# Moving state-space parameters, squares and states in the mixer of a hybrid decoder layer

## The chip, the cores and the metric

The kernel runs on one core of a Trainium2 chip. The metric is the device time of one execution in microseconds; the times shown are medians of several runs.

## The reference

One decoder layer on 1024 tokens of width 1024, in float32. A vector c gives six modulation rows; x is normalized and modulated, and `proj = hn @ w_in` feeds two mixers side by side, gated linear attention (GLA) and a diagonal state-space model (S5). A mixture of experts (4 of 32) follows.

```python
mod = jax.nn.silu(c) @ ada_w[l] + ada_b[l]
sh1, sc1, g1, sh2, sc2, g2 = jnp.split(mod, 6, axis=-1)
hn = rmsnorm(h, mix_pre_g[l]) * (1.0 + sc1[:, None, :]) + sh1[:, None, :]
proj = hn @ w_in[l]
q, k, v, og, a_lr, u = jnp.split(proj, SPLITS, axis=-1)
...
# s5_layer(u, ...): per group of 16 channels, 64 complex states
dt = jnp.exp(log_dt)[:, None]
mag = jnp.exp(lr * dt)
ab_re = mag * jnp.cos(li * dt); ab_im = mag * jnp.sin(li * dt)
...
_, _, xr, xi = lax.associative_scan(combine, (a_re, a_im, bu_re, bu_im), axis=1)
y = einsum(xr, c_re) - einsum(xi, c_im) + d * uf
y = jax.nn.gelu(y); s5 = y * jax.nn.sigmoid(y @ glu_w + glu_b)
...
h = h + g1 * rmsnorm(jnp.concatenate([gla, s5]) @ w_out, mix_post_g)
h = h + g2 * rmsnorm(moe_ffn(rmsnorm(h, ffn_pre_g) * (1 + sc2) + sh2), ffn_post_g)
```

## The kernel before, in words

Every engine runs its instructions in the order in which the program issues them, and so do the queues from which SP, ACT and POOL issue transfers; semaphores hold an instruction until what it reads is there and until what it overwrites has been read. The tile `S` is one large buffer which `view` cuts into places by hand; many places serve several things one after the other.

**Modulation rows.** `ada_row(i, mod_c, on_v)` (line 289) is a generator. Each of its eight steps issues one load of 512 KB from SP into the next of six buffers (`ada_r`, line 240) and uses it: TensorE multiplies it by c (`product`, four passes), or, for the k listed in `on_v`, VectorE multiplies it into `acc` (line 306 for the first, line 308 for the others; helpers at 143 and 148), which TensorE sums later. A last step turns the row into columns. `rows[0]` has `on_v` = (2, 5), `rows[1]` has (1, 3, 5). Load number n waits until load n - 6 has been used; the ninth load (the first of `rows[1]`) follows the use of k = 2 of `rows[0]` on VectorE. `take(gen, n)` (line 650) advances a generator by n steps. After the loads of the rows SP issues x's blocks 0 to 3, `fetch(0)` (1 MB of w_in), `load_b`, x's blocks 4 to 7 and smaller loads.

**State-space parameters.** `s5_prep` (line 360) is a generator of nine steps of small VectorE operations (128x16): the exponential of dt, angle and exponential, sine and cosine, powers of the rotation (`u8a`, the end of step 4), and so on. `s5_rot` (line 480) builds the rotation tables `rot` from `u8a` with POOL, doubling the width n from 1 to 64; the last stage has twelve operations of 128x512. Lines 133, 136 and 139 are the helpers for multiplication, addition and subtraction on VectorE and POOL alike.

**x.** `x_half(q)` (line 730) takes four blocks of x, squares them on ACT with accumulators (line 733), and VectorE makes 1/rms (ten small operations) and the diagonal matrices `dg`. `x_cols(q, k)` (line 739) lets TensorE transpose and scale a column block with `dg` (line 744), ACT writes it twice (lines 747 and 748), and VectorE subtracts the low part (`hnl`). `tile_T(i, j, half, first)` (line 754) is a tile of 24 matmuls of 128x512 (line 768) on high and low parts; with `first` it calls `x_cols` for all eight k between its matmuls. `u_tile` (line 776) evacuates such a tile and, after the second half, writes it to `U_d` from ACT. The order is `u_tile(0,0,0,first)`, `x_half(1)`, `u_tile(0,1,0)`, `u_tile(0,0,1,first)`, `conv(1)`, `u_tile(0,1,1)`, `load_u(0)`, `u_tile(1,0,0)`, `u_tile(1,1,0)`, `u_tile(1,0,1)`, `u_tile(1,1,1)`, `load_u(1)`. `load_u` (line 784) reloads U from `U_d` from SP in another layout, eight transfers.

**The planner.** The order between these tiles and side work is made while the program is built, by counted costs. `now` is TensorE's planned time, `busy` VectorE's; `spend(us)` advances `now` and lets background generators (`background(gen, at)`) go on if they are due and `busy` is less than `look` ahead. A generator yields "v" (it costs VectorE so much), "pe" (TensorE), "lag" and "sync" (not before so much later). `finish(...)` issues all the rest of a generator at once, without regard to its lags. Side work is: `s5_g` (line 510: for each of eight h8, six multiplications and additions of 128x256 on VectorE, then transposes on TensorE), `s5_ca` (line 529: eight steps, each with a complex multiplication on VectorE into `ca`, four CA_d writes from SP, copies on ACT, products on TensorE into `kr` by a copy on ACT, eight T_d writes from SP; `ca` and `kr` exist once), and `s5_states(hf)` (line 573: for q = 0, 1: 32 products with U on TensorE (line 584), six operations on VectorE in the places r1, r2, zr, zi of C1, scans (line 599), six more, and four XY writes from SP (line 610) that read r1 and zi). `states(0)` starts 5 us of planned time after `u_tile(1,0,0)`; its end is forced by `finish(st_a)` (line 862), ahead of the gates (lines 867 to 900) and the k tiles. `finish(g_gate, g_m, g_st)` (line 975) issues what is left of `s5_ca` and `states(1)` ahead of the q tiles. `s5_outs` (line 621) makes four output groups and is ended by `finish(g_y)` (line 986).

```python
    def pump():
        ...
                while g[1] <= now[0] and busy[0] < now[0] + look[0] and step(g):
    ...
            st_a = states(0)
            background(st_a, now[0] + 5.0)
        u_tile(1, 1, half)
    load_u(1)
```

Of the kernel before, what the change touches and what calls it, by code (L numbers as in the profile page):

```python
# [16 lines left out]
AF = mybir.ActivationFunctionType  # L17
OP = mybir.AluOpType
# [7 lines left out]
EPS = 1e-6  # L26
RD = 1.0 / 32.0
# [21 lines left out]
def hybrid_layer_kernel(ctx: ExitStack, tc: tile.TileContext, I, out):  # L49
    nc = tc.nc  # L50
    V, A, P, PE, SP = nc.vector, nc.scalar, nc.gpsimd, nc.tensor, nc.sync
# [16 lines left out]
    def carve(base, kb, *dims):  # L68
        n = 1
        for d in dims:  # L70
            n *= d
        o = int(round(kb * 256))
        v = base[:, o:o + n]
        if len(dims) == 2:
            v = v.rearrange("p (a b) -> p a b", a=dims[0])
        elif len(dims) == 3:
            v = v.rearrange("p (a b c) -> p a b c", a=dims[0], b=dims[1])
        return v

    def view(kb, *dims, dt=F32):  # L80
        n = 1
        for d in dims:
            n *= d
        o = int(round(kb * 256))
        w = n if dt in (F32, F32R, I32, U32) else n // 2
        assert o + w <= int(SBKB * 256), (kb, dims)
        v = S[:, o:o + w]
        if dt != F32:
            v = v.bitcast(dt)
        if len(dims) == 2:  # L90
            v = v.rearrange("p (a b) -> p a b", a=dims[0])
        elif len(dims) == 3:
            v = v.rearrange("p (a b c) -> p a b c", a=dims[0], b=dims[1])
        elif len(dims) == 4:
            v = v.rearrange("p (a b c d) -> p a b c d", a=dims[0], b=dims[1], c=dims[2])
        return v
# [12 lines left out]
    def small(*dims, dt=F32):  # L109
        n = 1  # L110
        for d in dims:
            n *= d
        kb = small_at[0]
        small_at[0] += n / 256
        return view(kb, *dims, dt=dt)
# [7 lines left out]
    def trb(*dims):  # L123
        return bank("tr", 2, *dims)

    def axb(*dims):
        return bank("ax", 3, *dims)
# [13 lines left out]
    def ts(o, a, s1, op0, s2=None, op1=None, e=None):  # L141
        if op1 is None:
            (e or V).tensor_scalar(o, a, s1, None, op0=op0)  # L143
        else:
            (e or V).tensor_scalar(o, a, s1, s2, op0=op0, op1=op1)

    def stt(o, a, s, b, op0, op1, **kw):
        V.scalar_tensor_tensor(o, a, s, b, op0=op0, op1=op1, **kw)  # L148

    def bc(ap, axis, n):  # L150
        u = ap.unsqueeze(axis)
        shape = list(u.shape)
        shape[axis] = n
        return u.to_broadcast(shape)
# [9 lines left out]
    now, busy, look = [0.0], [0.0], [LOOK]  # L164
# [34 lines left out]
    def background(gen, at=0.0):  # L199
        gens.append([gen, at])  # L200
# [15 lines left out]
    TB = 64  # L216
# [132 lines left out]
    def cmul(o, x, y, t, neg_im=False, e=None):  # L349
        mul(t[0], x[0], y[0], e)  # L350
        mul(t[1], x[1], y[1], e)
        sub(o[0], t[0], t[1], e)
        mul(t[0], x[0], y[1], e)
        mul(t[1], x[1], y[0], e)
        if neg_im:
            stt(o[1], t[0], -1.0, t[1], OP.mult, OP.subtract)
        else:
            add(o[1], t[0], t[1], e)
# [121 lines left out]
    def s5_rot():  # L480

        for hf in range(2):
            for i in range(2):
                P.memset(rot[hf][i][:, :, 0:1], 1.0 - i)
        wk, wn, t16 = u8a, [small(16), small(16)], [small(16), small(16)]
        n = 1
        while n < 128:
            for hf in range(2):
                tr4 = [carve(C1, 2 * i, 8, n) for i in range(2)]
                gl = slice(8 * hf, 8 * hf + 8)  # L490
                ro = rot[hf]
                cmul([ro[i][:, :, n:2 * n] for i in range(2)], [ro[i][:, :, 0:n] for i in range(2)],
                     [bc(wk[i][:, gl], 2, n) for i in range(2)], tr4, e=P)
            if 2 * n < 128:
                cmul(wn, wk, wk, t16, e=P)
                wk, wn = wn, wk
            n *= 2
# [123 lines left out]
    def s5_outs():  # L621
        y8 = [C1[:, 1024 * i:1024 * i + 1024].rearrange("p (a b c) -> p a b c", a=4, b=2)
              for i in range(2)]

        load_tc(1)
        yield "lag", 2.0
        for Q in range(4):
            hf = Q // 2
            for g2 in range(2):
                yp = axb(4, 128)  # L630
                for j in range(4):
                    gl = 2 * j + g2
                    PE.matmul(yp[:, j], T8[Q % 2][:, gl], U16[:, 8 * Q + gl], start=True, stop=False)
                    PE.matmul(yp[:, j], C8[Q % 2][:, gl], XY[hf][g2][:, 4 * (Q % 2) + j], start=False, stop=True)
                A.activation(y8[Q % 2][:, :, g2], yp, AF.Gelu_apprx_tanh)
                yield "pe", 1.8
            for t_ in range(8):
                A.dma_start(bass.AP(tensor=Y_d.tensor, offset=Y_d.offset + Q * 128 * 1024 + t_ * 128,
                                    ap=[[1024, 16], [16384, 8], [1, 128]]),
                            y8[Q % 2][16 * t_:16 * t_ + 16].rearrange("p a b n -> p (a b) n"))  # L640
            yield "lag", 1.5
            if Q < 2:
                load_tc(Q + 2)
            yield "lag", 1.0 if Q == 0 else 3.0


    mod = small(16)
    prep = s5_prep()

    def take(gen, n=1):  # L650
        for _ in range(n):
            try:
                next(gen)
            except StopIteration:
                return
# [5 lines left out]
    vecs2 = view(TB + 2.5, 128)  # L661
    for nm, r_, n in (("s5_glu_b", 0, 4), ("b_alpha", 4, 2), ("gla_norm_g", 6, 1)):
        P.dma_start(vecs2[r_:r_ + n], I[nm][0].rearrange("(a b) -> a b", b=128))
    take(prep)
    take(rows[0], 5)
    take(prep)
    p0 = trb(24)
    PE.transpose(p0, vecs[0:24], ident[0:24, 0:24])
    V.tensor_copy(vt, p0)
# [4 lines left out]
    glub, balpha, glag = vt2[:, 0:4], vt2[:, 4:6], vt2[:, 6:7]  # L674
    take(rows[0], 2)
    take(rows[1], 2)
    take(prep)
    take(rows[0])
    a1 = small(8)
    stt(a1, mod[:, 8:16], 1.0, vt[:, 16:24], OP.add, OP.mult)  # L680
    take(prep)
    s5_rot()
    X0, X1 = slot("E0"), slot("E1")
    xa = [view(R2 + 4 * b, 1024) for b in range(4)] + [carve(X0, 0, 1024), carve(X0, 4, 1024), carve(X1, 0, 1024),
                                                       carve(X1, 4, 1024)]
# [35 lines left out]


    sst, rx, tx, hx_ = small(8), small(8), small(8), small(8)
    dg = view(R0 + 14, 4, 128)
    hx_r = [view(TB, 512), view(TB + 2, 512)]
    hnh = [t_[:, 0:1024] for t_ in HN]
    hnl = [t_[:, 1024:2048] for t_ in HN]
    n_hx = [0]

    def x_half(q):  # L730
        c4 = slice(4 * q, 4 * q + 4)
        for b in range(4 * q, 4 * q + 4):
            A.activation(view(TB, 1024), xa[b], AF.Square, scale=RD, accum_out=sst[:, b:b + 1])
        ts(sst[:, c4], sst[:, c4], EPS, OP.add)
        rsqrt(rx[:, c4], sst[:, c4], tx[:, c4], hx_[:, c4])
        mul(dg, bc(ident, 1, 4), bc(rx[:, c4], 2, 128))
        vec(2.0)

    def x_cols(q, k):
        cols = slice(512 * q, 512 * q + 512)  # L740
        n_hx[0] += 1
        pt = (trb, axb)[n_hx[0] % 2](4, 128)
        for b in range(4):
            PE.matmul(pt[:, b], xa[4 * q + b][:, k * 128:(k + 1) * 128], dg[:, b], start=True, stop=True)
        pt = pt.rearrange("p a b -> p (a b)")
        hx = hx_r[n_hx[0] % 2]
        A.activation(hx, pt, AF.Identity, bias=mod[:, k:k + 1], scale=a1[:, k:k + 1])
        A.activation(hnh[k][:, cols], pt, AF.Identity, bias=mod[:, k:k + 1], scale=a1[:, k:k + 1])
        sub(hnl[k][:, cols], hx, hnh[k][:, cols].bitcast(F32))
        vec(0.6)  # L750
        spend(0.87)


    def tile_T(i, j, half, first=False):

        hi, lo = wparts[i]
        o = mmb(512)
        cols = slice(512 * half, 512 * half + 512)
        c_ = slice(128 * j, 128 * j + 128)
        n = 0  # L760
        if first:
            for k in range(3):
                x_cols(half, k)
        for k in range(8):
            if first and k < 5:
                x_cols(half, k + 3)
            for a_, b_ in ((hi, hnh), (hi, hnl), (lo, hnh)):
                PE.matmul(o, a_[:, k, c_], b_[k][:, cols], start=(n == 0), stop=(n == 23))
                n += 1
            if k % 2:  # L770
                spend(1.3)
        return o
# [75 lines left out]
    for half in range(2):  # L848
        u_tile(1, 0, half)
        if half == 0:  # L850
            conv(2)
            fetch(3)
            st_a = states(0)
            background(st_a, now[0] + 5.0)
        u_tile(1, 1, half)

    load_u(1)
# [583 lines left out]
    for blk in range(2, 8):  # L1441
        oo, xt = [mmb(512), axb(512)], load_x(blk)
        routes.append(route(blk, oo, xt))
        q = blk - 1
# [574 lines left out]
```

## Time and profile before

| | |
|---|---|
| median of 3 runs | 2021.15 us (2018.4 to 2021.25) |
| the profiled execution, its own time | 2024.69 us |
| its span, first to last instruction | 2022.9 us |
| busy share of the span | PE 89%, weight loads 80%, DVE 76%, ACT 59%, POOL 26% |
| mean granted TensorE clock | 0.948 of full speed |
| DMA | 540.82 MB, mean 267 GB/s |

Times in the rows below are microseconds from the span's start; of one instruction in a group some are given in ns. PE is TensorE's matmul row, DVE VectorE, ACT ScalarE, POOL GpSimd, and SPq the queue from which SP issues transfers (its durations are those of the issue, not of the transfer). A line of the timeline merges instructions that follow each other: start, time, engine, line, operation, what it writes and reads, how many, and in brackets the idle time of the engine before it and what ended it.

### The profile page before, as it was taken

Reading aid. Unit: us, or ns where it says so; the run is one execution under the profiler, and the core shown is the slowest. Engines: PE = TensorE matmul, PEld = TensorE weight load, DVE = VectorE, ACT = ScalarE, POOL = GpSimd, SP = SyncE. Lnnn points to the kernel's source line nnn. Section 1 sums busy time; section 2 is a strip of 40 time slices with the busy share of each in tenths; the row PEclk is TensorE's granted clock in tenths of the full one; section 3 lists DMA queues with packets and bytes.
Section 4 is the critical chain, followed back from the end, with each engine's and each line's share of the span. In section 5 each row is a group of like instructions: output and inputs, shape, how many; then the busy total and the mean of one; then the engine's idle time right before and its main releaser. Section 6 shows DMA issues by size and latency. Waiting matters only on the chain. (4 is left out here: it accounts for less than half of the span.)

```text
span 2022.9 us, 53263 instructions
## 1 busy us (share of the span) xinstructions
PE 1806.0 (89%) x22354; PEld 1614.5 (80%) x22354; DVE 1544.2 (76%) x2396; ACT 1199.1 (59%) x1682; POOL 526.5 (26%) x495
## 2 busy tenths in 40 slices
PE   8678699998968999998998899999899889999970
PEld 3566588787858999998998899767799789999870
DVE  5766537568767997995997799689799868869835
ACT  3524133544226876875776677577688667768641
POOL 4720012203543025015104402400330330160043
PEclk8889899999978999999999899999999989999985
DMA  9176465323359999999999899888999999999874
GB/s 310 39 193 132 137 196 161 126 70 131 115 172 326 363 322 353 379 351 307 323 329 358 278 351 341 279 323 301 299 367 365 301 296 330 327 318 350 306 192 175
DMA packets 296804, 540.82 MB, mean 267 GB/s; under 512 B 41234, under 2 KB 66032, under 8 KB 296528
## 3 DMA queue, kind: packets, MB, share of 16 engines
q1 hardware_dynamic: 259504, 469.51, 67.5%
q0 software_dynamic: 30384, 60.49, 11.8%
q10 hardware_dynamic: 6672, 7.38, 1.1%
q8 instruction: 177, 2.90, 0.6%
q14 instruction: 67, 0.55, 0.1%
HBM read 489.57 MB, written 45.61 MB: 265 GB/s over the span
## 5 line engine op out<-in xcount | busy, mean ns | idle before, releaser
L1765 POOL DMA_INDIRECT ff_d<-A,S x102 | 260.7, 2555 | 353.8 <-DVE A L143 141.2
L1588 DVE SCALAR_TENSOR_TENSOR B<-A,B 128x2048 f16<-128x2048 f32 x110 | 249.5, 2285 | 33.1 <-ACT B L1585 21.0
L1588 DVE SCALAR_TENSOR_TENSOR E<-A,E 128x2048 f16<-128x2048 f32 x110 | 249.7, 2285 | 16.0 <-ACT E L1585 15.8
L1726 POOL DMA_INDIRECT S<-hn_d,S x51 | 77.8, 1526 | 702.2 <-PE tr L1736 661.7
L1588 DVE SCALAR_TENSOR_TENSOR C<-A,C 128x2048 f16<-128x2048 f32 x110 | 249.7, 2284 | 8.3 <-ACT C L1585 8.2
L1585 ACT ACTIVATE B<-A 128x2048 f16<-128x2048 f32 x110 | 209.2, 1917 | 46.7 <-DMA A<-in_exp_w_gu_dram 36.7
L1585 ACT ACTIVATE E<-A 128x2048 f16<-128x2048 f32 x110 | 208.9, 1917 | 33.1 <-DMA A<-in_exp_w_gu_dram 18.4
L1585 ACT ACTIVATE C<-A 128x2048 f16<-128x2048 f32 x110 | 208.7, 1920 | 25.9 <-PE ax L1792 15.3
L1791 PE MATMUL mm<-S,E 128*128 128x92 f16 (+29 forms) x1336 | 187.8, 230 | 0.6 <-issue 0.5
L1791 PE MATMUL mm<-S,B 128*128 128x164 f16 (+28 forms) x1364 | 185.3, 227 | 3.3 <-issue 3.2
L1792 PE MATMUL mm<-S,B 128*128 128x164 f16 (+28 forms) x1364 | 184.9, 227 | 3.8 <-issue 3.8
L1792 PE MATMUL mm<-S,E 128*128 128x92 f16 (+29 forms) x1336 | 187.5, 229 | 0.0
L1792 PE MATMUL mm<-S,C 128*128 128x92 f16 (+28 forms) x1352 | 183.0, 226 | 3.2 <-issue 3.0
L1791 PE MATMUL mm<-S,C 128*128 128x92 f16 (+28 forms) x1352 | 183.2, 227 | 1.7 <-ACT S L1602 1.7
L1791 PEld LDWEIGHTS <-B 128*128 128x128 f16 x1760 | 154.3, 98 | 16.8 <-issue 9.4
L1791 PEld LDWEIGHTS <-C 128*128 128x128 f16 x1760 | 153.3, 98 | 13.0 <-issue 6.3
L1791 PEld LDWEIGHTS <-E 128*128 128x128 f16 x1760 | 155.0, 98 | 9.6 <-issue 2.0
L1792 PEld LDWEIGHTS <-B 128*128 128x128 f16 x1760 | 154.2, 98 | 9.4 <-issue 2.1
L1792 PEld LDWEIGHTS <-E 128*128 128x128 f16 x1760 | 154.9, 98 | 7.9 <-issue 0.4
L1792 PEld LDWEIGHTS <-C 128*128 128x128 f16 x1760 | 153.0, 98 | 8.3 <-issue 1.8
L148 DVE SCALAR_TENSOR_TENSOR S<-S 128x1 f32<-128x1 f32 (+7 forms) x249 | 106.0, 434 | 42.2 <-DMA S<-in_ada_w_dram 28.4
L1588 DVE SCALAR_TENSOR_TENSOR A<-A,A 128x2048 f16<-128x2048 f32 x54 | 123.5, 2286 | 3.1 <-ACT A L1585 2.9
(353 smaller groups left out, 4266.7 us busy)
## 6 DMA issues: line engine op xcount, KB each, us to landing
A<-in_exp_w_gu_dram SPq DMA_DIRECT2D x256, 1024.0 KB
A<-in_exp_w_down_dram SPq DMA_DIRECT2D x128, 1024.0 KB
S<-in_ada_w_dram POOLq DMA_DIRECT2D x64, 256.0 KB
S<-in_ada_w_dram SPq DMA_DIRECT2D x16, 512.0 KB
S<-in_w_in_dram SPq DMA_DIRECT2D x8, 1024.0 KB
S<-in_x_dram SPq DMA_DIRECT2D x12, 512.0 KB
ff_d<-S POOLq DMA_DIRECT2D x18, 256.0 KB
S<-in_w_out_dram SPq DMA_DIRECT2D x8, 512.0 KB
```

The costliest lines, as they stand in the source:

```text
L148: V.scalar_tensor_tensor(o, a, s, b, op0=op0, op1=op1, **kw)
L1585: A.activation(WH[n % NWS], ST[n % NST], AF.Copy, scale=WS)
L1588: V.scalar_tensor_tensor(WL[n % NWS], ST[n % NST], WS, WH[n % NWS], op0=OP.mult, op1=OP.subtract, accum_out=acc_col())
L1726: lambda e: P.indirect_dma_start(out=x_[0:cb], out_offset=None, in_=hn2_d, in_offset=bass.IndirectOffsetOnAxis(ap=x.lt[0:cb, b, 0:1], axis ...
L1765: lambda e: P.indirect_dma_start(out=ff_d[c], out_offset=bass.IndirectOffsetOnAxis(ap=x.lt[0:cb, b, 0:1], axis=0), in_=yt[0:cb], in_offset ...
L1791: PE.matmul(pp[q], w_, mh[:, f_], start=(f_ == 0 and q % per == 0), stop=False, skip_group_check=True)
L1792: PE.matmul(pp[q], w_, ml[:, f_], start=False, stop=False, skip_group_check=True)
```

## The change

Steps 2 to 4 of `s5_prep` and `s5_rot` are issued ahead of the steps of `rows[0]` that follow its first load. The squares of x's blocks 4 to 7 become eight half squares with accumulators of their own (`sst2`), issued on ACT behind the last `x_cols` of the first tile, with `hnh[7]`'s second half as their scratch; `x_half(1)` adds the two halves. `states(0)` starts 16 us of planned time after `u_tile(1,0,0)`. The lag behind the second output group of `s5_outs` is 10 instead of 3.

```diff
@@ s5_outs
-            yield "lag", 1.0 if Q == 0 else 3.0
+            yield "lag", (1.0, 10.0, 3.0, 3.0)[Q]
@@
-    take(prep)
+    take(prep, 4)
+    s5_rot()
     take(rows[0], 5)
-    take(prep)
     p0 = trb(24)
...
     take(rows[0], 2)
     take(rows[1], 2)
-    take(prep)
     take(rows[0])
     a1 = small(8)
     stt(a1, mod[:, 8:16], 1.0, vt[:, 16:24], OP.add, OP.mult)
-    take(prep)
-    s5_rot()
@@
+    sst2 = small(2, 4)
...
+    def x_squares():
+
+        for b in range(4, 8):
+            for i in range(2):
+                A.activation(hnh[7][:, 512:1024], xa[b][:, 512 * i:512 * i + 512], AF.Square, scale=RD,
+                             accum_out=sst2[:, i, b - 4:b - 3])
+
     def x_half(q):
         c4 = slice(4 * q, 4 * q + 4)
-        for b in range(4 * q, 4 * q + 4):
-            A.activation(view(TB, 1024), xa[b], AF.Square, scale=RD, accum_out=sst[:, b:b + 1])
-        ts(sst[:, c4], sst[:, c4], EPS, OP.add)
+        if q:
+            stt(sst[:, c4], sst2[:, 0], EPS, sst2[:, 1], OP.add, OP.add)
+        else:
+            for b in range(4):
+                A.activation(view(TB, 1024), xa[b], AF.Square, scale=RD, accum_out=sst[:, b:b + 1])
+            ts(sst[:, c4], sst[:, c4], EPS, OP.add)
@@ tile_T
             if first and k < 5:
                 x_cols(half, k + 3)
+            if first and half == 0 and k == 4:
+                x_squares()
@@
             st_a = states(0)
-            background(st_a, now[0] + 5.0)
+            background(st_a, now[0] + 16.0)
```

## Rows read from the trace of the kernel before

**Rows 1.** Busy time by stretch: engines, granted clock, DMA share, GB/s; the start.

```profile
0.00:22.60 22.60, 17.61 (x37) 3.27 (x37) 10.28 (x61) 2.49 (x4) 2.76 (x13) 1.00 0.86 308
22.60:34.60 12.00, 11.00 (x33) 3.46 (x34) 9.26 (x50) 4.15 (x8) 4.90 (x15) 0.86 1.05 386
```

**Rows 2.** Timeline, TensorE: the first products on x.

```profile
42.28 2.08 PE L744 MATMUL ax<-S 128*128 128x128 f32 x8
```

**Rows 3.** Timeline, SP's queue: loads of the modulation's weights, merged and one alone.

```profile
2.43 11.63 SPq L300 DMA_DIRECT2D S<-in_ada_w_dram  x9
...
12.53 0.33 SPq L300 DMA_DIRECT2D S<-in_ada_w_dram  x1
```

**Rows 4.** Groups of instructions, POOL, 75.2 to 92.1 us: count, busy us, mean ns.

```profile
L133 POOL TENSOR_TENSOR C<-E,S 128x512 f32<-128x512 f32 x8 | 10.3, 1310 | 0.2
```

**Rows 5.** Groups, VectorE, 81.5 to 89.4 us and 102 to 115 us.

```profile
L133 DVE TENSOR_TENSOR S<-S 128x256 f32<-128x256 f32 x4 | 5.2, 1347 | 0.0
...
L133 DVE TENSOR_TENSOR S<-S 128x256 f32<-128x256 f32 x16 | 6.1, 421 | 0.2
```

**Rows 6.** Timeline, 28 to 98 us: rotation, squares, second half, its evacuation.

```profile
28.78 0.21 POOL L133 TENSOR_TENSOR C<-E,S 128x8 f32<-128x8 f32 x1 [25.28 <-DVE S L139]
...
62.14 1.05 ACT L733 ACTIVATE S<-E 128x1024 f32<-128x1024 f32 x1
...
66.86 0.18 DVE L143 TENSOR_SCALAR S<-S 128x4 f32<-128x4 f32 x1 [3.07 <-ACT S L733]
...
71.79 1.28 PE L744 MATMUL ax<-S,E 128*128 128x128 f32 x8 [4.26 <-DVE S L133]
...
97.61 0.60 ACT L158 ACTIVATE S<-mm 128x512 f32<-128x512 f32 x1 [3.99 <-PE mm L768]
```

**Rows 7.** Busy time by stretch: U's reload, and its second half with XY.

```profile
120.60:132.00 11.40, 0.01 (x2) 0.03 (x1) 3.11 (x9) 1.94 (x5) 0.00 (x0) 0.64 1.18 178
162.00:174.50 12.50, 11.56 (x64) 8.94 (x63) 7.29 (x14) 9.47 (x13) 0.00 (x0) 1.00 1.10 121
```

**Rows 8.** Timeline, 118 to 165 us: CA_d writes, first states, second states, gates.

```profile
125.14 3.65 SPq L550 DMA_DIRECT2D CA_d<-S  x4
...
132.00 3.68 PE L584 MATMUL ax<-S 128*64 128x128 f32 x32 [11.39 <-DMA S<-U_d]
...
153.40 1.29 DVE L133 TENSOR_TENSOR C<-ax,E 128x512 f32<-128x512 f32 x2
...
163.89 1.40 DVE L145 TENSOR_SCALAR S<-mm,S 128x512 f32<-128x512 f32 x2
```

**Rows 9.** Timeline, 160 to 240 us: load_u(1), T_d writes, exponentials, XY's wait, q tiles.

```profile
160.67 5.29 SPq L786 DMA_DIRECT2D S<-U_d  x8
...
170.59 5.45 SPq L565 DMA_DIRECT2D T_d<-S  x8
...
173.45 1.92 ACT L888 ACTIVATE E<-E 128x2048 f32<-128x2048 f32 x1
...
206.06 3.83 SPq L565 DMA_DIRECT2D T_d<-S  x8
...
213.01 3.79 SPq L565 DMA_DIRECT2D T_d<-S  x8
...
218.74 20.70 PE L768 MATMUL mm<-A,E 128*128 128x512 f32 x90
...
227.91 1.29 DVE L133 TENSOR_TENSOR C<-ax,E 128x512 f32<-128x512 f32 x2 [3.17 <-DMA S<-C]
```

**Rows 10.** Timeline, VectorE, 14 to 29 us: operations of steps 2 to 4 of s5_prep.

```profile
14.95 0.25 DVE L133 TENSOR_TENSOR S<-S 128x16 f32<-128x16 f32 x2
...
17.93 0.18 DVE L669 COPY S<-tr 128x24 f32<-128x24 f32 x1
...
21.48 1.30 DVE L148 SCALAR_TENSOR_TENSOR S<-S 128x16 f32<-128x16 f32 x12
...
25.64 0.75 DVE L133 TENSOR_TENSOR S<-S 128x16 f32<-128x16 f32 x5
```

## The prediction

> **What bounds the kernel now.** I read the trace by stretches. The change touches the first 245 us of a 2022.9 us span, the mixer; what follows starts when the mixer is done, so I take a shift there as a shift of the end. Four limits follow one another in this stretch.
>
> The first 42 us belong to the transfers: from 22.6 to 34.6 us the DMA engines are full and move 386 GB/s [rows 1], and TensorE's first product on x comes at 42.28 us [rows 2]. SP issues nine loads of the modulation's weights between 2.43 and 14.06 us, and one of them, the first of the second row, at 12.53 us [rows 3]: it goes into the buffer that held load k = 2 of the first row, which VectorE must have multiplied before.
>
> From 42 to 98 us VectorE is shared with POOL. Beside POOL's last stage of the rotation tables, twelve operations of 128x512 from 75.2 to 92.1 us, eight of them at 1.31 us [rows 4], a 128x256 operation of VectorE takes 1.35 us; some 20 us later, with POOL idle, 0.42 us [rows 5]. VectorE waits once for the squares of x's second half, 3.07 us [rows 6].
>
> From 120.6 to 132 us TensorE does nothing [rows 7]: the states' products wait 11.39 us for U's reload, and VectorE waits behind them. From there VectorE runs nearly without a gap through the second states' multiplications at 153.40 us to the gates' first operation at 163.89 us [rows 8].
>
> From 170 to 213 us the limit is the chain of s5_ca's eight steps: the copy into kr waits until the T_d writes of the step before have read it. The last two steps, with little other work between them, stand 6.95 us apart (206.06 and 213.01 us) [rows 9].
>
> **Parameters and rotation ahead of the rows.** Nothing is added; steps 2 to 4 of s5_prep, 61 small VectorE operations, now stand ahead of the rows' multiplications. Step 2 lasts from 14.95 to 17.93 us (2.98), step 3 about 2.2 (twelve of its 18 operations take 1.30), step 4 from 25.64 us [rows 10] to about 29.1 (3.5; POOL takes its result at 28.78 us [rows 6]): together 8.7 us. So VectorE reaches load 2 some 8.7 us later, and SP's load behind it, with all that is queued after it (x, w_in, load_b), goes out at 12.53 + 8.7 = 21.2 us. Until then only eight loads of 0.524 MB are out, 4.19 MB; before, 308 GB/s for 22.6 us had moved 6.96 MB [rows 1]. The missing 2.77 MB cost 7.2 us at 386 GB/s; I take **7.0** (bounds 4, if gaps of before are filled, to 8.7, SP's whole delay). The second row and w_in land by so much later, and x's first product moves from 42.28 to 49.3 us.
>
> POOL starts the rotation when step 4 is done, at 20.5 instead of 28.78 us [rows 6]. VectorE's 1024-wide products of the rows, which POOL waits for, now fall inside it: I take 2.7 us of the 8.2 as lost (an estimate). Its last stage then runs from about 70 to 86.6 us. Behind the tables POOL has nothing queued before 102 us.
>
> **Squares within the first tile.** Eight half squares with their accumulators replace four whole ones on ACT. The half form is not in the trace; the whole one takes 1.05 us [rows 6], so eight cost 4.2 to 8.4; I take 6. They lie beside the tile's last products, when ACT has no more work for the tile; were they late, x_half(1) would wait as now. The gain is at most the 3.07 us of VectorE's wait. I give it nothing: in VectorE's order the six multiplications of s5_g(0) stand ahead of x_half(1), and they now fall into POOL's last stage. From 70 us VectorE still has there one subtraction, those six and the diagonal, eight at 1.31 us, and ten small operations, which I put at 0.6 (0.17 alone, as in step 4, and 1.31 if each waits for one of POOL's): 16.5 us. x's second half starts at 86.9 instead of 71.79 us [rows 6]. Its tile then runs without POOL: of the 25.8 us to the evacuation at 97.61 us [rows 6], six multiplications save 5.6 us and two subtractions some 1.7, so it ends at 105.4 us: **+7.8** in all, 0.8 beyond the start's delay (bounds -5, if POOL holds VectorE less, to +3).
>
> The Trainium skill ("SBUF — State Buffer", Who interferes with whom) says that a VectorE operation with two SBUF inputs and a GpSimd operation take the shared port as an exclusive lock, and the second to issue blocks fully. The 1.35 us agree. By that rule the ten small operations would cost 13 us instead of 6, but POOL ends first, and the sum would be about 1 us higher.
>
> **The states later.** Adding up the planner's own costs (spend, vec, the yields), the first states' product moves from ahead of all of u_tile(1,0,1) to behind it and half of u_tile(1,1,1), and behind steps 0 and 1 of s5_ca. In the times of before, without the shift so far: TensorE goes on at 120.6 us, step 0's products run at 124. Step 1 must overwrite ca, which step 0's CA_d writes still read; they are issued from 125.14 us behind U's reload, which lands at 132.0 [rows 8], and a 1 MB load, 2.6 us at 386 GB/s: 134.5. So step 1's products come at 136 to 139, the states' at 139 to 141.5. TensorE has gained some 8 us there, VectorE under 1: it has the same work left.
>
> Now the new wait. On SP, load_u(1) is now issued ahead of the first states' four XY writes; before, it came after them. It waits for u_tile(1,1,1): twelve more matmuls to 144.3, evacuation and write to 148.4 us. Before, from load_u(1)'s first issue at 160.67 us [rows 9] the queue carried U and the next XY until 174.5 us at 121 GB/s [rows 7]: 13.8 us. So XY lands at about 162.3. The second states' first multiplication overwrites what XY reads; the trace shows that wait elsewhere (3.17 us at 227.91 us [rows 9]). It ran at 153.40 us [rows 8] and now at 162.7: **+9.3** on VectorE, and so on the gates' operation behind it, which frees TensorE's banks. Bounds: 0, if XY lands in time, to 10.
>
> The new order also puts step 2's products behind the gates' exponentials, whose last one ends at 175.4 us [rows 9], now 184.7; two subtractions of VectorE later, step 2's T_d comes at 187 instead of 170.59 us [rows 9]. Then 42 matmuls at 0.23 us (20.70 us for 90 [rows 9]) stand ahead of step 3, 9.5 us, and the other four steps follow each other at 6.95: 187 + 9.5 + 27.8 = 224.3 against 213.01 us, **+11.3** (bounds -8, the wait of 11.39 gone and 3 given back, to +15). What is late next: the second states, and with them the outputs, as now.
>
> **The lag of 10 in s5_outs.** By the planner's costs output 0 goes out within the last q tile, and finish(g_y) issues the rest without regard to lags. The order doesn't change: 0. Were that cover gone, outputs 2 and 3 would stand behind the q tiles, where they already are.
>
> **Sum.** 7.8 + 11.3 = 19 us. The profiled execution took 2024.69 us, 3.5 above the median of 2021.15; the sum is a difference, and on the median it gives 2040. A measurement of this kernel can tell about 0.2% (4 us) from no change.
>
> **The rivals.**
> *Gain in the states (other side).* XY does not hold VectorE, and s5_ca, which starts 11 us earlier, stays ahead: -8. The start's 7 are met by the squares (-3) and by POOL, which ends before the second tile (-5): -1. Total -9: 2012. For it speaks that TensorE's largest wait goes; against it VectorE's queue, full from the states on. It decides where the second states' multiplication starts: at once behind its queue, or after an idle stretch. Chance 0.17.
> *Only the start.* The states' move changes where TensorE waits, and s5_ca ends as before: 2021.15 + 7.8 = 2029. For it: that chain hangs on SP's writes, not on TensorE. Chance 0.20.
> *XY overtakes U.* XY's data do not stand behind U's, and only its issue is late: 148.4, 5.29 for load_u(1)'s issues [rows 9], and some 5 for its own and the landing (an estimate), 158.7: 5.3 instead of 9.3, so 2036. The 13.8 us of U and XY together speak against it, but don't separate them. Chance 0.10. The Trainium skill ("DMA: Bandwidth & Descriptors", Queues, rings and completion order) says that descriptors are consumed in ring order on each engine, yet completion is not first-in first-out for an issuing engine; no row here decides it.
> *Wash.* The start costs 7, the states give 6 back: 2022. Chance 0.08.
> *The forecast:* 0.45; by itself 2032 to 2047 (start 4 to 8.7, states 7 to 15).
>
> **How the numbers follow.** Slower by over 0.2%: 0.45 + 0.20 + 0.10 = 0.75; same 0.08; faster 0.17. The range has to reach past the wash into the gain: 2015 to 2047 leaves out some 0.12 below and 0.06 above.
>
> **What would show it.** Right: the ninth load issued near 21 us and the DMA engines idle from about 15 to 22; x's first product near 49, the second half's near 87; XY issued behind load_u(1), and VectorE idle for several us ahead of the second states' multiplication; TensorE without work between the last steps of s5_ca, and its last T_d about 19 us later than now. Wrong: the ninth load before 16 us (the start then costs nothing), the second half's product before 80 us, or a last T_d at or before 213 us.

## The result and the profile after

The changed kernel takes 2046.95 us (median of 4 runs, 2043.56 to 2056.01), the kernel before beside it 2021.2: ratio 1.0129, 95% interval 1.0087 to 1.0171. It is slower, as forecast; 25.75 us between the medians lie at the upper end of the range (2047), 2 us above what the forecast's two upper bounds add up to (8.7 and 15), where the sum had 19. The profiled execution took 2043.56 us, 18.9 more than that of before; it was the fastest of its four, and that of before stood 3.5 us above its median. Since the single runs of either kernel spread over 10 to 12 us, the size is taken up again in the first experiment. One of e6's twelve executions below took 5647.89 us, the only slow one, and its median is that of the other eleven.

"First" and "second states" in the prediction are the two halves (q = 0, 1) of `states(0)`; below they are called its first and second half. conv(1) splits a block of w_in into a high part, copied by ACT, and a low part, which VectorE subtracts (128x1024).

From the page of after, its span and its busy time:

```profile
span 2041.8 us, 53271 instructions
...
PE 1812.1 (89%) x22354; PEld 1617.8 (79%) x22354; DVE 1544.4 (76%) x2396; ACT 1198.9 (59%) x1690; POOL 517.6 (25%) x495
```

VectorE and ACT are busy as long as before (1544.2 and 1199.1 us there), TensorE 6 us longer (1806.0): the span grew mainly by waiting. By stretch (engines, granted clock, DMA share, GB/s), the start and the stretch in which TensorE had waited for U:

```profile
0.00:22.60 22.60, 12.37 (x25) 2.14 (x26) 13.37 (x86) 1.46 (x2) 5.03 (x18) 0.94 0.57 193
22.60:34.60 12.00, 12.00 (x35) 3.50 (x34) 3.40 (x6) 2.88 (x5) 10.04 (x44) 0.82 1.00 397
120.60:132.00 11.40, 10.99 (x59) 9.22 (x59) 7.89 (x18) 5.75 (x13) 1.24 (x4) 1.00 1.10 275
```

The first 22.6 us move 193 GB/s instead of 308 [rows 1], and TensorE now works through the stretch in which it had done nothing [rows 7]. SP's queue, in its order:

```profile
2.44 19.30 SPq L300 DMA_DIRECT2D S<-in_ada_w_dram  x9
...
20.93 0.80 SPq L300 DMA_DIRECT2D S<-in_ada_w_dram  x2
...
120.57 7.97 SPq L796 DMA_DIRECT2D S<-U_d  x8
...
130.89 3.70 SPq L550 DMA_DIRECT2D CA_d<-S  x4
...
156.38 4.00 SPq L796 DMA_DIRECT2D S<-U_d  x8
160.48 21.37 SPq L610 DMA_DIRECT2D C<-C  x8
...
225.69 3.59 SPq L565 DMA_DIRECT2D T_d<-S  x8
...
232.55 3.83 SPq L565 DMA_DIRECT2D T_d<-S  x8
```

The ninth load is issued at 20.93 us (12.53 before [rows 3]), load_u(1) now stands ahead of all eight XY writes, and the last T_d comes at 232.55 instead of 213.01 us [rows 9], 19.5 later. TensorE (x's first product, x's second half, the states' first half, the gates):

```profile
48.52 2.08 PE L752 MATMUL ax<-S 128*128 128x128 f32 x8
...
85.51 1.06 PE L752 MATMUL ax<-S,E 128*128 128x128 f32 x8
...
146.51 1.97 PE L584 MATMUL ax<-S 128*64 128x128 f32 x32
...
180.63 2.07 PE L891 MATMUL mm<-S 128*128 128x512 f32 x2 [12.72 <-DVE S L145]
```

VectorE, from conv(1)'s subtraction on:

```profile
104.95 2.36 DVE L139 TENSOR_TENSOR E<-S,E 128x1024 fp32r<-128x1024 f32 x2 [2.16 <-ACT E L158]
...
121.51 2.36 DVE L139 TENSOR_TENSOR B<-S,B 128x1024 fp32r<-128x1024 f32 x2 [1.44 <-ACT B L158]
...
131.43 0.23 DVE L136 TENSOR_TENSOR S<-S 128x64 f32<-128x64 f32 x1 [2.40 <-ACT S L158]
...
141.41 0.46 DVE L139 TENSOR_TENSOR S<-S 128x288 f32<-128x288 f32 x1 [9.01 <-DMA CA_d<-S]
...
148.42 0.23 DVE L136 TENSOR_TENSOR S<-S 128x64 f32<-128x64 f32 x1 [5.14 <-ACT S L158]
...
151.26 1.28 DVE L133 TENSOR_TENSOR C<-ax,E 128x512 f32<-128x512 f32 x2
...
161.14 0.69 DVE L136 TENSOR_TENSOR C<-C 128x512 f32<-128x512 f32 x1
...
169.34 1.29 DVE L133 TENSOR_TENSOR C<-ax,E 128x512 f32<-128x512 f32 x2 [7.51 <-DMA C<-C]
...
179.83 2.06 DVE L145 TENSOR_SCALAR S<-mm,S 128x512 f32<-128x512 f32 x3
```

The same engine in the kernel before, in the same stretch:

```profile
116.28 2.36 DVE L139 TENSOR_TENSOR B<-S,B 128x1024 fp32r<-128x1024 f32 x2 [1.44 <-ACT B L158]
...
135.29 1.29 DVE L133 TENSOR_TENSOR C<-ax,E 128x512 f32<-128x512 f32 x2 [11.47 <-PE ax L584]
...
140.37 0.23 DVE L136 TENSOR_TENSOR S<-S 128x64 f32<-128x64 f32 x1 [1.02 <-ACT S L158]
...
150.34 0.23 DVE L136 TENSOR_TENSOR S<-S 128x64 f32<-128x64 f32 x1 [0.53 <-ACT S L158]
```

These brackets are the heart of the result. From the subtraction at 121.51 us (116.28 before) to the second half's first multiplication VectorE now waits 1.44 + 2.40 + 9.01 + 5.14 + 7.51 = 25.5 us; before, 1.44 + 11.47 + 1.02 + 0.53 = 14.5. The wait for U is gone and three others have come: for the CA_d writes of s5_ca's step 0, for ACT's copy into kr, for XY. The difference, 11.0 us, and the 5.2 us by which conv(1)'s subtraction is late (99.75 before) add up to 16.2, against the 15.9 us by which that multiplication moved (153.40 to 169.34 us). TensorE's wait has moved too: 11.39 us for U before [rows 8], 12.72 us for VectorE at the gates now.

### The profile page after: what moved, and what is told of

Read it like the earlier page. It is cut to its first block, busy times and chain, and to the rows that moved or that the text cites. A ratio compares the mean times of both kernels' runs of the same rounds, so it can differ in the third digit from the quotient of the medians.

```text
span 2041.8 us, 53271 instructions
## 1 busy us (share of the span) xinstructions
PE 1812.1 (89%) x22354; PEld 1617.8 (79%) x22354; DVE 1544.4 (76%) x2396; ACT 1198.9 (59%) x1690; POOL 517.6 (25%) x495
## 5 line engine op out<-in xcount | busy, mean ns | idle before, releaser
L1736 POOL DMA_INDIRECT S<-hn_d,S x51 | 71.3, 1397 | 706.8 <-PE tr L1746 597.5
L148 DVE SCALAR_TENSOR_TENSOR S<-S 128x512 f32<-128x512 f32 (+8 forms) x250 | 108.5, 442 | 42.8 <-DMA S<-in_ada_w_dram 27.5
```

Of the source, the lines that this page charges most:

```text
L1736: lambda e: P.indirect_dma_start(out=x_[0:cb], out_offset=None, in_=hn2_d, in_offset=bass.IndirectOffsetOnAxis(ap=x.lt[0:cb, b, 0:1], axis ...
```

## The experiments

Each kernel was timed beside the kernel before; e1 to e4, e5 to e8 and e9 to e11 share one series of it each, and e12 has its own. Times of the profile are those of one execution: x's first product, conv(1)'s subtraction, the first multiplications of the two halves of `states(0)`, and the issue of the last step's T_d.

| run | median, us | before beside it | ratio, 95% interval | x | conv(1) | half 1 | half 2 | last T_d |
|---|---|---|---|---|---|---|---|---|
| before | | | | 42.28 | 99.75 | 135.29 | 153.40 | 213.01 |
| after | 2046.95 | 2021.2 | 1.0129 (1.0087 to 1.0171) | 48.52 | 104.95 | 151.26 | 169.34 | 232.55 |
| e1 after again | 2043.12 | 2024.72 | 1.0113 (1.0079 to 1.0147) | 48.82 | 104.26 | 151.52 | 170.55 | 233.58 |
| e2 rows back | 2039.48 | 2024.72 | 1.0075 (1.0047 to 1.0103) | 41.33 | 96.91 | 144.14 | 161.87 | 225.06 |
| e3 states back | 2034.71 | 2024.72 | 1.0053 (1.0032 to 1.0073) | 48.87 | 104.22 | 138.15 | 155.45 | 213.97 |
| e4 XY first | 2039.16 | 2024.72 | 1.0084 (1.0058 to 1.0111) | 48.86 | 104.73 | 149.76 | 163.56 | 226.26 |
| e5 states back | 2033.73 | 2025.4 | 1.0044 (1.0023 to 1.0066) | 49.01 | 106.04 | 140.53 | 157.48 | 217.39 |
| e6 squares only | 2023.53 | 2025.4 | 0.9990 (0.9976 to 1.0005) | 42.69 | 97.52 | 134.00 | 151.45 | 211.25 |
| e7 load free | 2022.6 | 2025.4 | 0.9997 (0.9979 to 1.0016) | 40.04 | 96.03 | 130.00 | 147.44 | 207.12 |
| e8 CA_d by ACT | 2044.27 | 2025.4 | 1.0092 (1.0065 to 1.0119) | 48.76 | 104.68 | 149.15 | 167.47 | 230.50 |
| e9 CA_d, T_d by ACT | 2043.91 | 2025.56 | 1.0071 (1.0053 to 1.0089) | 49.06 | 105.99 | 147.80 | 165.10 | 228.37 |
| e10 all three | 2033.25 | 2025.56 | 1.0031 (1.0014 to 1.0049) | 41.79 | 99.07 | 141.59 | 155.31 | 218.40 |
| e11 U in two queues | 2021.27 | 2025.56 | 0.9965 (0.9947 to 0.9983) | 40.65 | 97.80 | 132.62 | 149.26 | 207.71 |
| e12 load free | 2022.44 | 2025.29 | 0.9995 (0.9969 to 1.0021) | 42.06 | 99.00 | 132.60 | 149.52 | 208.47 |

**e1, the changed kernel again** (no edit).

> The changed kernel once more, timed in five rounds beside the one before. Theory: the loss is what the two profiles show in the mixer, 18.9 us, so the medians stand 17 to 21 us apart (ratio 1.0084 to 1.0104). Rival: some 7 us more arise behind the mixer, and the medians stand 24 to 28 us apart again (ratio 1.012 to 1.014). What tells it in the profile: the last T_d issue near 232.5 us, and the span behind it longer or not than the 1809.9 us of before.

18.4 us between the medians is the theory's number, but the ratio, 1.0113, lies between the theory's range and the rival's, and its interval holds both. The last T_d is 20.6 us later than before, and the execution profiled here ended only 13.9 us later (span 2036.8 against 2022.9): behind the mixer single executions drift by several us either way. The interval puts the loss at 16 to 30 us (0.0079 and 0.0147 of 2025), which holds the first 25.75 as well.

**e2, parameters and rotation back in their places.**

```diff
-    take(prep, 4)
-    s5_rot()
+    take(prep)
     take(rows[0], 5)
+    take(prep)
@@ (the two other take(prep) and s5_rot() as before)
```

> Steps 2 to 4 of s5_prep and the rotation go back to their places of before; squares and states stay as changed. Theory: the ninth load is issued at 12.5 us again, x's first product comes at 42.3 us, the second half's between 70 and 73 us (VectorE's 3.07 us wait for squares gone), and all that follows is 5 to 8 us earlier than in the changed kernel; against the kernel before it stays 11 to 15 us slower. Rival: the early rotation pays for the late load by freeing VectorE from POOL; then this is no faster than the changed kernel, within 2 us.

x's first product came at 41.33 us, the second half's at 69.53, the last T_d 7.5 to 8.5 us ahead of the changed kernel's. The median gained only 3.6 us, and the intervals of e1 and e2 overlap; against the kernel before the median stands 14.8 us higher, as the theory had it. The early rotation does not pay for the late load in the traces; the times alone would not have said so.

**e3 and e5, the states back at 5 us** (one kernel, measured twice).

```diff
-            background(st_a, now[0] + 16.0)
+            background(st_a, now[0] + 5.0)
```

> states(0) starts at 5 us of planned time again; the rest stays as changed. Theory: the states' part of the loss, 14.3 us in the profile, goes; the last T_d comes at 213.0 + 5.2 = 218.2 us, and the kernel is 5 us slower than the one before (4 to 8). Rival: the loss in the states is the start's delay carried on and grown, and this kernel stays over 12 us slower than the one before.

> states(0) at 5 us again, once more: its first profile showed the mixer's end 1.4 us later than before and the shortest of its twelve times, while the median stood 10 us above that of before. Theory: the mixer swallows the start's delay each time (last T_d 213 to 215 us), the median is 0 to 5 us above the one before, and a first look of 10 us was scatter of what runs behind the mixer. Rival: in other executions the start's 5 us go through the mixer (last T_d 217 to 219 us), or something behind it grows, and the median is 8 to 12 us above again.

The states' move costs more than anything else: without it the last T_d falls from 233 to 214 and 217 us. But e3's theory of a 5 us rest and e5's of a swallowed start both fail: the medians stay 10.0 and 8.3 us above before, as e5's rival had it. The two profiles show why a single one misleads. In e3's execution the 4.5 us by which conv(1) was late had shrunk to 1.0 at the last T_d, and the span was 1.7 us shorter than before's (2021.2); in e5's, 6.3 had become 4.4, and the span was 9.1 us longer (2032.0). The medians follow the second.

**e4, XY ahead of load_u(1).** The order on every engine but SP is that of the changed kernel.

```diff
+    finish(st_a)
     load_u(1)
...
     background(g_st, now[0])
-    finish(st_a)
```

> One edit on the changed kernel: the first states are ended ahead of load_u(1), so that SP issues their four XY writes ahead of load_u(1)'s eight transfers; nothing else changes its order on any engine. Theory: the second states' first multiplication loses its 7.5 us wait for XY and comes at 160 to 163 us instead of 169.3; the last T_d comes 7 to 10 us earlier (223 to 226), and the kernel is 8 to 11 us faster than the changed one. Rival: XY is late because VectorE makes r1 and zi late, not because of its place on SP, or U's reload, now behind XY, takes the wait's place on TensorE; then the time is that of the changed kernel within 3 us.

SP's queue (XY, all eight writes together) and VectorE in e4:

```profile
158.30 17.78 SPq L610 DMA_DIRECT2D C<-C  x8
```

```profile
163.56 1.29 DVE L133 TENSOR_TENSOR C<-ax,E 128x512 f32<-128x512 f32 x2 [3.23 <-DMA C<-C]
```

The wait for XY falls from 7.51 to 3.23 us, not to nothing: the rest is XY's own issue and landing. The issue itself was not late: in both kernels SP had issued XY's last write some 2 us behind VectorE's last operation (at 163.97 us in after, at 162.33 in e4). From there to the multiplication it took 5.4 us in after and 1.2 in e4. So 4.3 us of the wait were U's data ahead of XY's in SP's queue, and the rival that XY overtakes U is out. The Trainium skill ("DMA: Bandwidth & Descriptors", Queues, rings and completion order) says that descriptors are consumed in ring order on each engine; the 5.4 and 1.2 us agree. The last T_d is 6 to 7 us earlier, the median 4 us. The theory named the right queue and gave it twice its share.

**e6, the squares alone**, and the lag, in the kernel before.

```diff
-            yield "lag", 1.0 if Q == 0 else 3.0
+            yield "lag", (1.0, 10.0, 3.0, 3.0)[Q]
@@ tile_T (with x_squares and x_half as in the change)
+            if first and half == 0 and k == 4:
+                x_squares()
```

> The kernel before with the squares moved (and the lag of 10), nothing else. Theory: VectorE's wait of 3.07 us goes, x's second half starts 1 to 2.5 us earlier (69.3 to 70.8 us), conv(1)'s subtraction 2 to 3 us earlier, and the time is 0 to 3 us less than before, since the mixer passes on only part of a shift of its start. Rival: the eight half squares with their reads of the accumulators take 6 us of ACT where four took 4.8, and delay the first tile's evacuation; then x's second half is no earlier and the time is the same or 1 to 2 us more.

Ratio 0.9990, not to be told from no change. In the trace the move works: the wait of 3.07 us [rows 6] is gone, conv(1) is 2.2 us and the last T_d 1.8 us earlier, and eight half squares with their reads take 6 us of ACT, as assumed. Apart from the squares and the first of the small operations behind them, every engine runs the same instructions in the same order as before, so the lag of 10 changes no order. ACT and VectorE in e6:

```profile
58.65 0.63 ACT L735 ACTIVATE A<-E 128x512 fp32r<-128x512 f32 x1
```

```profile
65.01 0.69 DVE L148 SCALAR_TENSOR_TENSOR S<-S 128x4 f32<-128x4 f32 x1
...
68.54 0.54 DVE L148 SCALAR_TENSOR_TENSOR S<-S 128x4 f32<-128x4 f32 x1
```

The sum of the squares' halves at 65.01 us has no wait in front of it.

**e7 and e12, the load freed** (states at 5 us, measured twice).

```diff
-    take(prep, 4)
-    s5_rot()
+    take(prep)
     take(rows[0], 5)
+    take(prep, 3)
+    s5_rot()
@@
-            background(st_a, now[0] + 16.0)
+            background(st_a, now[0] + 5.0)
```

> The states back at 5 us, and the rows' five steps issued ahead of steps 2 to 4 of s5_prep, with the rotation right behind these: the rotation stays early, and the ninth load no longer waits for s5_prep. Theory: the ninth load goes out at 12 to 13 us, x's first product comes at 42 to 44 us (48.9 with the load held), the rotation ends 3 to 8 us earlier than before, conv(1)'s subtraction at 94 to 98 us, and the time is 0 to 4 us below the one before. Rival: what delays x is the rotation beside the rows' products on VectorE, not the held load: then x's first product stays past 46 us.

> The kernel with the load freed and the states at 5 us once more, without the split of U's reload. Theory: its mixer ends 4 to 6 us earlier than that of before, the split added nothing to it (there the states' first multiplication came later, at 132.6 us instead of 130.0), and the time is 2 to 6 us below the kernel before (ratio 0.997 to 0.999). Rival: the split is what made the split kernel faster, and this one stays within 1 us of the kernel before.

The start by stretch, SP's queue and x's first product in e7:

```profile
0.00:22.60 22.60, 16.40 (x36) 2.97 (x36) 12.49 (x80) 3.20 (x5) 2.77 (x13) 1.00 0.89 323
```

```profile
12.18 0.93 SPq L300 DMA_DIRECT2D S<-in_ada_w_dram  x2
```

```profile
40.04 1.16 PE L753 MATMUL ax<-S 128*128 128x128 f32 x8
```

The rotation is still early (its last stage ends at 85.8 and 83.6 us, 92.0 before), the ninth load leaves at 12.2 us, and x's first product comes at 40 to 42 us. Against e3 and e5, which differ from it only in this order, the median falls by 11 us. So the held load, not the rotation beside the rows' products, is the loss at the start. Against e6, which differs only in the place of steps 2 to 4 and the rotation, the last T_d comes 2.8 to 4.1 us earlier, but the ratio is no lower (0.9997 and 0.9995 against 0.9990): no run shows in the time what the early rotation gains. Against before the last T_d is 4.5 to 5.9 us earlier and the medians 2.8 us lower both times, but the intervals hold 1. e12's median stands as its theory had it, its ratio (0.9995, 1 us) as its rival had it; it does not decide between them.

**e8 and e9, step 0's writes by ACT.** In e8 the CA_d writes, in e9 those of T_d as well; all else as in the changed kernel.

```diff
-                    SP.dma_start(CA_d[...], ca[i][...])
+                    (SP if s8 else A).dma_start(CA_d[...], ca[i][...])
@@ (e9 alone)
-                SP.dma_start(T_d[...], kr[...])
+                (SP if s8 else A).dma_start(T_d[...], kr[...])
```

> One edit on the changed kernel: the four CA_d writes of s5_ca's step 0 are issued by ACT instead of SP, where they stand behind U's reload and a 1 MB load. Theory: they go out before 128 us and land by 135 instead of 141.4; VectorE's wait of 9.01 us for them shrinks to under 4; the first states and all behind them come 4 to 7 us earlier, and the kernel is 4 to 7 us faster than the changed one. Rival: the writes are slow because U's reload and the load fill the DMA engines, or the next wait (ACT's copy into kr, the first states' products) takes their place: then less than 2 us.

> The changed kernel with the CA_d and the T_d writes of s5_ca's step 0 both issued by ACT; moving CA_d alone had left ACT's copy into kr waiting 10.4 us for T_d. Theory: the states' first half used to cover the landing of these two writes, which stand on SP behind U's reload and a 1 MB load; with both off SP, VectorE's waits there (9.01 and 5.14 us in the changed kernel) fall under 4 together, the states' first multiplication comes at 140 to 145 us instead of 151.3, and the kernel is 6 to 11 us faster than the changed one. Rival: these writes are slow on any queue while U's reload runs, or the wait goes on to a third place; then the time stays within 3 us of the changed one.

VectorE, ACT and SP in e8:

```profile
134.56 0.46 DVE L139 TENSOR_TENSOR S<-S 128x288 f32<-128x288 f32 x1 [1.63 <-DMA CA_d<-S]
...
145.94 0.23 DVE L136 TENSOR_TENSOR S<-S 128x64 f32<-128x64 f32 x1 [9.51 <-ACT S L158]
```

```profile
145.25 0.66 ACT L158 ACTIVATE S<-tr 128x256 f32<-128x256 f32 x2 [10.40 <-DMA T_d<-S]
```

```profile
121.45 12.29 SPq L796 DMA_DIRECT2D S<-U_d  x8
...
134.52 9.12 SPq L565 DMA_DIRECT2D T_d<-S  x8
```

The wait for CA_d falls from 9.01 to 1.63 us, so those writes were slow for their place on SP, not because the DMA engines were full; but ACT's copy into kr then waits 10.40 us for T_d, which still stands on SP behind U's reload and 1 MB of w_in, and the time stays (the rival). The Trainium skill ("DMA: Bandwidth & Descriptors", Queues, rings and completion order) says that each DMA engine takes turns between the queues that have work for it; the 1.63 us agree. VectorE in e9:

```profile
140.79 0.23 DVE L136 TENSOR_TENSOR S<-S 128x64 f32<-128x64 f32 x1 [4.35 <-ACT S L158]
...
146.02 0.46 DVE L139 TENSOR_TENSOR S<-S 128x288 f32<-128x288 f32 x1 [4.26 <-DMA CA_d<-S]
...
165.10 1.29 DVE L133 TENSOR_TENSOR C<-ax,E 128x512 f32<-128x512 f32 x2 [6.73 <-DMA C<-C]
```

With both moved, 0.3 us are left for the CA_d of step 0, 4.35 us for kr and 4.26 us for the CA_d of step 1, still on SP: a third place. The states' first half begins at 147.8 us, 3.5 earlier, not at 140 to 145, and the last T_d 4 to 5 us earlier. The ratio falls from e1's 1.0113 to 1.0071, while the medians stand 18.4 us apart in both and the intervals overlap: a few us at most.

**e10, all three losses taken away** (e9's edit, e4's, and the load freed as in e7; the states stay at 16 us).

> The changed kernel with all its suspected losses taken away together: CA_d and T_d of step 0 by ACT, XY ahead of load_u(1), and the rows' five steps ahead of steps 2 to 4 of s5_prep. Theory: the ninth load, XY's place and the two writes are the whole loss; the last T_d comes at 205 to 215 us and the time within 5 us of the kernel before, on either side. Rival: the late order of the states costs by itself (VectorE has the same work and starts it later), and some 8 us or more above the kernel before stay.

VectorE in e10:

```profile
128.98 0.46 DVE L139 TENSOR_TENSOR S<-S 128x288 f32<-128x288 f32 x1 [1.68 <-DMA CA_d<-S]
...
134.64 0.23 DVE L136 TENSOR_TENSOR S<-S 128x64 f32<-128x64 f32 x1 [3.79 <-ACT S L158]
...
139.80 0.46 DVE L139 TENSOR_TENSOR S<-S 128x288 f32<-128x288 f32 x1 [4.19 <-DMA CA_d<-S]
...
155.31 1.29 DVE L133 TENSOR_TENSOR C<-ax,E 128x512 f32<-128x512 f32 x2 [3.16 <-DMA C<-C]
```

7.7 us above before, 10.8 above e12, which has the same start with the states early. The rival is nearer: with these waits shortened the late order still costs some 10 us. In these two conv(1) comes at the same time (99.07 and 99.00 us), the last T_d 9.9 us apart. From the subtraction at 115.59 us to its second half VectorE still waits 17.5 us (the four brackets, 1.43 and 3.22), against 11.5 in e12, and from the gates' first operation to the last T_d it takes 52.6 us (165.80 to 218.40) against 48.5 in e12 (160.01 to 208.47).

**e11, U's first reload in two queues** (e7 with four of the eight transfers on ACT).

```diff
-            SP.dma_start(U16[...], ...)
+            (SP if s_ % 2 or hf else A).dma_start(U16[...], ...)
```

> The kernel with the load freed (states at 5 us), and four of the eight transfers of U's first reload issued by ACT instead of SP. Theory: the reload is held by its issues, 8 us for eight on one queue; in two queues it lands 2 to 4 us earlier, the states' first multiplication, now at 130.0 us, moves by as much, and the time falls by 1 to 4 us, 3 to 7 below the kernel before. Rival: the reload is bound by its round trip and small packets, or the mixer swallows the gain; then the time is that with the load freed within 2 us.

ACT and VectorE in e11:

```profile
119.65 0.66 ACT L158 ACTIVATE S<-tr 128x256 f32<-128x256 f32 x2 [12.69 <-DMA S<-U_d]
```

```profile
120.81 0.42 DVE L139 TENSOR_TENSOR S<-S 128x256 f32<-128x256 f32 x1 [10.30 <-PE tr L522]
```

The wait only moved: ACT, which now stands 7.0 us at its first issue until U_d is written and another 5.2 us over the four, keeps TensorE and VectorE waiting 9 to 10 us before 121 us, and the first half begins at 132.62 us, as in e12. Its mixer is no faster than those of e7 and e12, so the mechanism failed; yet it is the one kernel whose interval lies below 1 (0.9947 to 0.9983), 4.3 us under the kernel before. The freed load, the early rotation, the moved squares and the states in their old place are common to all three kernels, and its interval overlaps theirs; that the split adds to it is not shown.

## Why the prediction was right or wrong

**Direction and chain.** Right: slower, by a held load at the start and by the states' late place, with the last T_d 19.5 us later where the sum had 19. That this fits so well is luck: the start came out 2.6 us smaller than its 7.8, the states 3.0 larger than their 11.3. The size on the medians was 25.75 and, measured again, 18.4 us; 25.75 is 6.9 us more than the two profiles show, because the execution profiled of after lies 3.4 us below its median and that of before 3.5 above.

**The start's delay, 7.0.** Right in its mechanism to a fraction of a microsecond: the ninth load at 20.93 us (21.2 forecast), 193 GB/s until 22.6 us, x's first product at 48.52 us (49.3), 6.2 us later. e7 shows the cause.

**POOL and the second half, 0.8.** The step "I take 2.7 us of the 8.2 as lost" failed. The rotation began at 19.89 us and its last operation began at 77.86; the tables took 59.3 us where they had taken 63.3, so POOL ended at 79.2 us, not at 86.6. POOL and VectorE in after:

```profile
19.89 0.21 POOL L133 TENSOR_TENSOR C<-E,S 128x8 f32<-128x8 f32 x1 [16.39 <-DVE S L139]
...
77.86 1.33 POOL L136 TENSOR_TENSOR E<-C 128x512 f32<-128x512 f32 x1
```

```profile
81.11 0.16 DVE L148 SCALAR_TENSOR_TENSOR S<-S 128x4 f32<-128x4 f32 x1
...
82.69 0.16 DVE L148 SCALAR_TENSOR_TENSOR S<-S 128x4 f32<-128x4 f32 x1
82.96 1.37 DVE L133 TENSOR_TENSOR S<-S 128x512 f32<-128x512 f32 x3
```

The small operations, nine and not ten, then ran with POOL idle, in 1.7 us instead of the 6 put down for them; beside POOL's 128x256 stage, in e6, they took 4.1 (65.01 to 69.08 us), 0.45 each. So the 13 us worked out from the exclusive lock of the Trainium skill ("SBUF — State Buffer", Who interferes with whom) did not arise, and no run here put these operations beside POOL's last stage. x's second half came at 85.51 us (86.9), and conv(1) was 5.2 us late, not 7.8.

**The states, 11.3.** TensorE's side was right: with the 5.2 us of the start, step 1's products and the states' were to fall at 141 to 147 us, and the states' came at 146.51. The step that failed is "VectorE under 1: it has the same work left". It has, but it cannot do it. The sum had the landing of step 0's CA_d writes (134.5 us, 139.7 with the shift; the wait ends at 141.41), but no loss of VectorE from it, and nothing for T_d. Before, the first half's 10.6 us of VectorE work (151.26 to 161.83 us in after) stood where CA_d and T_d of step 0 land, and covered them; now that it stands behind steps 0 and 1, VectorE waits 2.40, 9.01 and 5.14 us there, 16.6 together, where it had waited 11.47 for U. That the second half is late by the shift and another 10.7 us (9.3 forecast) looks like a hit, but of the cause given, XY behind load_u(1), e4 leaves 4.3 us. The first half already begins 10.8 us late beyond the shift: 5.1 us of waits, and some 6 us for the multiplications of steps 1 and 2, which now stand ahead of it instead of between the first multiplications of the two halves. That they are gone from there, with 1.6 us of waits, gives back what XY's wait takes. Behind the gates another 3.6 us are lost, where the sum had 2. In the profile the whole term was 14.3 us instead of 11.3. Between e2 and e6, which differ only in the states, it is 13.8 us at the last T_d.

**The squares and the lag.** Both as priced, nothing: 0.9990 for the two together in e6, where the second changes no engine's order of instructions.

**The rivals.** "Only the start" is e3 and e5 by construction, 8.3 and 10.0 us for its 7.8; but the chain s5_ca does depend on the states' place. "XY overtakes U" falls with e4. "Gain in the states" falls with e10: even with its three waits shortened the late order ends behind. The wash had the states give back 6; they took 14.

**Open.** The parts measured alone, some 10 us for the start and 15 for the states, add up to more than the 18.4 us of e1, if to no more than its interval allows. And the start costs 8 to 10 us in the medians, where the two profiles show 1.0 and 4.4 at the last T_d; e5's was 9.1 us late at the end of the span, so something behind the mixer adds to it. There the step "I take a shift there as a shift of the end" does not hold. The times go with the granted clock: in e3's twelve executions its mean over the execution falls from 0.947 in the shortest (2022.95 us) to 0.942 in the longest (2040.83), and its median is 0.944 and 0.945 in e3 and e5, 0.947 in the kernel before beside them. Behind the last T_d the clock stood at the lower of its two levels (1.2 GHz) for 165 us in e3's profile, where that stretch took 1807.2 us, and for 176 in e5's, where it took 1814.6 (before: 165 and 1809.9). Whether the clock is the cause, and why it stood low for longer, no run shows.

## What to carry to other kernels

A wait is worth what the engine behind it does meanwhile. Before moving work out of a wait (here TensorE's 11.39 us for U), list for the engine that sets the end which landings this work was covering; they become its next waits. And in a program of queues in order, look at what a moved step's predecessors hold: here one product on VectorE stood between SP and the loads of the second row, of x and of w_in, and putting the five row steps back in front of 61 small operations took 11 us off.

## What the runs showed of the hardware beyond that

The issue of a group of transfers takes longer where its queue is backed up. Eight T_d writes took 3.59 us to issue with no reload ahead and 9.12 us behind U's reload in e8; U's own eight took 7.97 us in after, and 12.29 in e8 and 15.45 in e9, where ACT's writes ran beside them. In e9:

```profile
121.64 15.45 SPq L796 DMA_DIRECT2D S<-U_d  x8
```

A long issue on SP is thus no measure of the group alone: it grows with what stands ahead of it or runs beside it.

One program's stages shift by microseconds between executions: the same kernel had conv(1) at 104.22 and 106.04 us and its last T_d at 213.97 and 217.39 (e3, e5), and the first product on x moved by 2 us in the kernel of e7 and e12 (40.04 and 42.06). Differences of a few microseconds between single traces are of that size.
